# A gated delta rule on one core: the chunks' inverses applied to the decayed keys beforehand

## The chip, the core and the metric

The kernel runs on one core of a Trainium2 chip. A core has a matrix engine (TensorE, PE in the profile; PEld is its weight load, which overlaps the matmuls), three vector-like engines (VectorE or DVE, ScalarE or ACT, GpSimd or POOL), SyncE (SP), which issues most transfers, and 16 DMA engines that move data between device memory and the on-chip memory. Matmuls write to PSUM, a small memory of banks; DVE and ACT read the results from there. Each engine works through its own queue in order, and engines wait for one another by semaphores. The metric is device time in microseconds (us) for one launch.

## The reference, cut to what matters

The program is one step of a decoder layer for a prompt of 512 tokens (with 16 learned meta tokens ahead of it) and for eight sampled sequences of 8 tokens each. It has a differential attention, a gated delta rule, a merge of both by gates, and a convolutional feed-forward part. The change is in the delta rule, whose recurrence over chunks is this:

```python
lower = where(strict, einsum('cd,ed->ce', kb, kc) * decay, 0)
a_mat = lower + eye(chunk)
rhs = concatenate([vc * beta, kb * exp(gcum)], axis=-1)
sol = triangular_solve(a_mat, rhs, lower=True, unit_diagonal=True)
u, w = sol[..., :dv], sol[..., dv:]

def step(s, xs):
    v_new = u_i - w_i @ s
    intra = (q_i @ k_i.T) * dec_i
    o = (q_i * exp(g_i)) @ s + intra @ v_new
    s = s * exp(g_last) + (k_i * exp(g_last - g_i)).T @ v_new
    return s, o
```

There are four heads, each with keys and values of 128 elements. `v_new` is the inverse of `a_mat` applied to (values - decayed keys times state). The inverse can be applied to the difference, or to both of its terms; the reference does the second.

## The kernel before, in words

The kernel takes the prompt in chunks of 128 tokens (not 64 as the reference does), four per head, with the small inverse of each chunk built on the chip. The eight samples and the meta tokens form a fifth, shorter tile of 80 rows, called the tail, which is handled ahead of the four chunks and gives the first state `S`.

The projections are split into high and low parts and run as three matmuls each (`ps_d`, `ps_t`, `ps_g` and `ps_s` in the profile are the PSUM banks by tag, which late stages share). The delta rule's own small products are plain f32 matmuls, and each shows as two records.

The Python generators are streams: each `yield` hands over to another stream, and `yield DELAY[n]` says how much estimated work (in us) should be issued before the stream goes on. `merge` takes the stream that is furthest behind its weight and whose delay has passed. `main()` runs the prompt's attention, then `gdn`, then `mix_parts`; `rest()` runs the attention of the samples over the paged cache (page loads by SP, transpositions, scores, and products with `page` tiles) and then 16 gate projections (L1483). In `gdn`, the chain of head h (`gdn_chain`) is merged with the projections of head h+1 (`gdn_project`, with the convolution on DVE). For head 3 there is no next projection. The tile framework sets the waits, assigns the buffers, and may put an instruction that is ready ahead of others on its engine: for example the next head's `gu` (L714, POOL) runs in the solve of the head before it.

The steps of `gdn_chain` in order: `gu` and the decays (L714 to L745), transpositions and scaling of keys and values into `kn` and `vn` (L756 to L785), transposition of the keys into `kk` (L792, L796), the keys scaled for the state update in place as `kp` (L798 on DVE for the tail, L799 on POOL for the chunks), the scaled queries `qs` (L803, L804), the base blocks of the inverse (`gdn_base`), the doubling of the blocks (`gdn_solve`, which leaves the transposed inverse in `res["y"][:, i, 1]`), the tail, and then the chunk loop. In that loop, per chunk: the state times the keys, `kk` x `S`, in a bank; on DVE the negative decay and the values make `rhs` (L878); the inverse times `rhs`; a copy on ACT to `v` (L888); the state update `kp` x `v` and its sum on DVE (L893); and the two products of the output in a bank, read by ACT (L899) and DVE (L900). In chunk 1, `states()` puts the samples' state updates in between (L870 on DVE). After the loop POOL issues the state's transfer (L903) and computes a root for the output norm (`gf`, L376), after which the outputs are scaled, transposed and gated.

Buffers that matter here: `dd` is one tile per head pool (used by `gu`, by the decay differences, and by the solve), `on` is one tile (the outputs, five slots), `grhs`, `gv` and `gS` have two each, and the PSUM tag g has two banks in this stage.

Of the kernel before, what the change touches and what calls it, by code (L numbers as in the profile page):

```python
# [13 lines left out]
ALU = mybir.AluOpType  # L14
# [39 lines left out]
def _lay_out_constants():  # L54
# [78 lines left out]
DELAY = (  # L133
    10.08, 5.4, 0.6, 0.6, 6.0, 1.3, 0.9, 0.85, 1.32, 1.0, 1.68, 0.17, 26.0, 0.67, 2.93, 0.77,
    0.09, 0.85, 0.38, 2.28, 0.05, 1.54, 0.74, 1.56, 6.12, 0.84, 1.4, 11.52, 1.4, 1.68, 10.28,
)
# [14 lines left out]
class Body:  # L151
# [550 lines left out]
    def gdn_chain(self, h, st):  # L702
        nc, pool, a, o = self.nc, self.gpool, self.a, self.o
        q, kt, vt = st["q"], st["kt"], st["vt"]
        C4 = [128, 4, 128]

        def cols(ap, h=h):
            return ap[:, 0:4, h : h + 1].to_broadcast(C4)
# [6 lines left out]
            out=gu, in0=self.c("upper").unsqueeze(1).to_broadcast(C4), in1=cols(self.g), op=ALU.mult  # L715
# [9 lines left out]
        for big, sign in (("big_low", -1.0), ("big_up", 1.0)):  # L725
            m = self.t(pool, [NTL, NTL], "dt" + big)
            nc.vector.scalar_tensor_tensor(
                out=m, in0=rt[:NTL, :NTL], scalar=self.gc[:NTL, 4, h : h + 1], in1=self.c(big + "_t", NTL),
                op0=ALU.subtract, op1=ALU.add,
# [6 lines left out]
        dd = self.t(pool, C4, "dd")  # L736
# [13 lines left out]
        kn = self.t(pool, [128, 5, 128], "kn")  # L750
        vn = self.t(pool, [128, 5, 128], "vn")
# [20 lines left out]
        for i in range(4):  # L772
# [5 lines left out]
            out=rr, in0=rr, in1=self.mhalf[:, :10].rearrange("p (a b) -> p a b", a=2), op=ALU.pow  # L778
# [7 lines left out]
            out=kn[:, 0:4], in0=kn[:, 0:4], in1=kc[:, 0:4].unsqueeze(2).to_broadcast(C4), op=ALU.mult  # L786
        )
        yield DELAY[4]
        p = self.ps("t")
        self.transpose(p[:, :NTL], kn[:NTL, 4])  # L790
        kk = self.t(pool, [128, NT], "kk")
        nc.scalar.copy(kk[:, CS:NT], p[:, :NTL])  # L792
        p = self.ps4("t")
# [2 lines left out]
        nc.scalar.copy(kk[:, 0:SEQ].rearrange("p (c t) -> p c t", c=4), p)  # L796
        kp = kn
        nc.vector.tensor_scalar(kp[:NTL, 4], kn[:NTL, 4], self.ek[:NTL, 4, h : h + 1], None, op0=ALU.mult)  # L798
        nc.gpsimd.tensor_tensor(out=kp[:, 0:4], in0=kn[:, 0:4], in1=cols(self.ek), op=ALU.mult)  # L799
        yield DELAY[5]  # L800

# [2 lines left out]
        nc.gpsimd.tensor_tensor(out=qs[:, 0:SEQ], in0=q[:, 0:SEQ], in1=er[:, 0:SEQ], op=ALU.mult)  # L804
        yield 0.0

        on = self.t(pool, [128, 5, 128], "on")
        so = self.t(pool, [128, 5], "so")
        nc.vector.memset(so, 1.0)
        res = {}  # L810
# [7 lines left out]
        y, at = res["yt"], res["att"]  # L818
        p = self.ps("g")
        for b in range(NB):  # L820
# [3 lines left out]
        rhs = self.t(pool, [128, 128], "grhs", bufs=2)  # L824
        nc.vector.scalar_tensor_tensor(
            out=rhs[:64], in0=p[:64, :128], scalar=self.neg_eg[:64, 4, h : h + 1], in1=vn[:64, 4],
            op0=ALU.mult, op1=ALU.add,
# [5 lines left out]
        p = self.ps("g")  # L833
# [4 lines left out]
        p = self.ps("g")  # L838
        self.mm(p[:, :128], kp[64:NTL, 4], v[64:NTL], start=True, stop=True)
        S = self.t(pool, [128, 128], "gS", bufs=2)  # L840
        nc.vector.tensor_copy(S, p[:, :128])
        p = self.ps("g")
# [5 lines left out]
            out=state,  # L848
            in0=state,
            in1=last[:, 4:12].unsqueeze(2).to_broadcast([128, NB, 128]),  # L850
            op=ALU.mult,
        )
        vms = []
        for half in range(2):
# [3 lines left out]
                out=vm[:64],  # L858
                in0=v[:64].unsqueeze(1).to_broadcast([64, 4, 128]),
                in1=self.c("blocks_s", 64)[:, b4].unsqueeze(2).to_broadcast([64, 4, 128]),  # L860
                op=ALU.mult,
# [4 lines left out]
        def states():  # L866
            for b4, vm in vms:
                hp = self.ps4("g")
                self.mm(hp, kp[:64, 4], vm[:64].rearrange("p b v -> p (b v)"), start=True, stop=True)
                nc.vector.tensor_tensor(out=state[:, b4], in0=state[:, b4], in1=hp, op=ALU.add)  # L870


        for i in range(4):
            sl = slice(128 * i, 128 * i + 128)
            p = self.ps("g")
            self.mm(p[:, :128], kk[:, sl], S, start=True, stop=True)
            rhs = self.t(pool, [128, 128], "grhs", bufs=2)
            nc.vector.scalar_tensor_tensor(  # L878
                out=rhs, in0=p[:, :128], scalar=self.neg_eg[:, i, h : h + 1], in1=vn[:, i], op0=ALU.mult, op1=ALU.add
            )  # L880
            yield DELAY[9]
            if i == 1:
                states()
                yield 0.0
            p = self.ps("g")
            self.mm(p[:, :128], res["y"][:, i, 1], rhs, start=True, stop=True)
            v = self.t(pool, [128, 128], "gv", bufs=2)
            nc.scalar.copy(v, p[:, :128])  # L888
            yield DELAY[10]
            p = self.ps("g")  # L890
            self.mm(p[:, :128], kp[:, i], v, start=True, stop=True)
            S2 = self.t(pool, [128, 128], "gS", bufs=2)
            nc.vector.scalar_tensor_tensor(  # L893
                out=S2, in0=S, scalar=last[:, i : i + 1], in1=p[:, :128], op0=ALU.mult, op1=ALU.add
            )
            p = self.ps("g")
            self.mm(p[:, :128], qs[:, sl], S, start=True, stop=False)
            self.mm(p[:, :128], res["at"][:, i], v, start=False, stop=True)
            nc.scalar.activation(junk, p[:, :128], AF.Square, scale=cq[:, i : i + 1], accum_out=so[:, i : i + 1])  # L899
            nc.vector.tensor_copy(on[:, i], p[:, :128])  # L900
            S = S2
            yield DELAY[11]
# [7 lines left out]
            out=on[:, 0:4], in0=on[:, 0:4], in1=f[:, 0:4].unsqueeze(2).to_broadcast(C4), op=ALU.mult  # L910
# [4 lines left out]
        p = self.ps4("t")  # L915
# [4 lines left out]
        for dst, src in (((0, SEQ), p.rearrange("p c t -> p (c t)")), ((CS, CM), pt[:, 0:NS]), ((CM, NQ), pt[:, 78:80])):  # L920
            sl = slice(*dst)
            nc.vector.scalar_tensor_tensor(
                out=self.ob[:, h, sl], in0=src, scalar=self.gnorm, in1=z2[:, sl], op0=ALU.mult, op1=ALU.mult
# [878 lines left out]
```

## Time and profile before

| | us |
|---|---|
| median of 3 runs (1222.2 to 1225.16) | 1223.05 |
| the profiled execution | 1219.92 |
| its span, first to last instruction | 1218.2 |
| PE busy | 1168.2 (96%) |
| PEld busy | 1043.1 (86%) |
| DVE busy | 636.8 (52%) |
| ACT busy | 447.5 (37%) |
| POOL busy | 209.4 (17%) |

The mean granted TensorE clock is 0.992 of full speed. Busy times are those of one profiled execution. A matmul's end is modelled and matmuls overlap, so the distance between the starts of neighbours says more about PE's cost than the duration of one record. In rows grouped by line, the figures behind the bar are the busy time, the mean of one instruction in ns, and the idle time of the engine just before them with what ended it. In rows in order of time, the first number is the start, the second the duration (both in us), and the bracket at the end says how long the engine had been idle and what released it. The four chunk loops start at about 310, 404, 499 and 600 us.

### The profile page before, as it was taken

To read this page: it belongs to the slowest core of one execution; us is meant where nothing else is said; L and a number is where in the kernel's file an instruction comes from. 1 tells how busy PE (TensorE), PEld (TensorE's weight loads), DVE (VectorE), ACT (ScalarE), POOL (GpSimd) and SP (SyncE) were. 2 spreads that over 40 slices of the span, in tenths; PEclk is the share of its full clock that TensorE was granted. 3 is DMA by queue.
4 is the path that set the end of the run, shared out by engine and by line. 5 is a ranking of instruction groups with operands and counts; after the bars stand their busy time and mean duration, and the time that the engine had idled before them with its cause. 6 is when DMAs were issued, how large, how long until landed. Compare 5 with 4: busy or idle time off the path is not lost.

```text
span 1218.2 us, 24892 instructions
## 1 busy us (share of the span) xinstructions
PE 1168.2 (96%) x9439; PEld 1043.1 (86%) x9439; DVE 636.8 (52%) x1719; ACT 447.5 (37%) x1139; POOL 209.4 (17%) x341
## 2 busy tenths in 40 slices
PE   6999999989989989999999999999999999999996
PEld 5887787677677686679999987899999999999996
DVE  5456657586397497454226753455545545422224
ACT  5234444343333343342324433433333333323322
POOL 2122221150250241230100002321111111100000
PEclk9999999999999999999999999999999999999998
DMA  6374435726836657463232552322223223352222
GB/s 196 77 233 153 125 90 159 268 72 190 280 110 213 186 181 247 159 189 72 68 87 72 151 169 79 102 81 85 75 86 88 85 75 87 105 157 79 79 81 84
DMA packets 185006, 157.63 MB, mean 129 GB/s; under 512 B 13234, under 2 KB 147315, under 8 KB 184867
## 3 DMA queue, kind: packets, MB, share of 16 engines
q1 hardware_dynamic: 179569, 147.53, 40.0%
q0 software_dynamic: 4288, 5.16, 1.5%
q10 hardware_dynamic: 1030, 3.35, 0.8%
q8 instruction: 74, 1.21, 0.4%
q14 instruction: 45, 0.37, 0.1%
HBM read 146.12 MB, written 9.88 MB: 128 GB/s over the span
## 4 chain that ended last, share of the span: by engine, by line
PE 76%; DVE 7%; issue 6%; DMA 4%; ACT 3%; POOL 3%; DVEq 0%; ACTq 0%; POOLq 0%
PE ps_d L264 31%; PE ps_g L264 15%; PE ps_t L264 12%; PE ps_s L264 10%; PE ps_t L412 7%; DMA page<-in_cache_v 1%; PE ps_m L264 1%; DVE cy L640 1%; ACT KT L1388 1%; DMA wraw<-in_w_out 1%; DVE wlo L307 1%; DVE KT L1388 1%; DVE vt L647 1%; DMA wraw<-in_w_ffn_in 1%; DMA wraw<-in_w_in 0%
## 5 line engine op out<-in xcount | busy, mean ns | idle before, releaser
L307 DVE TENSOR_TENSOR wlo<-wraw,whi 128x512 fp32r<-128x512 f32 x238 | 159.0, 681 | 239.6 <-ACT whi L306 238.8
L306 ACT CAST whi<-wraw 128x512 fp32r<-128x512 f32 x240 | 143.1, 613 | 269.7 <-PE ps_d L264 106.5
L264 PE MATMUL ps_d<-xhi,whi 128*128 128x256 f32 (+2 forms) x704 | 219.7, 312 | 0.1
L264 PE MATMUL ps_d<-xhi,wlo 128*128 128x256 f32 (+2 forms) x704 | 215.0, 306 | 1.2 <-DVE wlo L307 1.2
L264 PE MATMUL ps_d<-xlo,whi 128*128 128x256 f32 (+2 forms) x704 | 215.2, 306 | 0.3 <-DVE xlo L307 0.2
L264 PEld LDWEIGHTS ps_d<-xhi,whi 128*128 128x128 f32 x704 | 135.3, 192 | 6.8 <-issue 4.6
L264 PEld LDWEIGHTS ps_d<-xhi,wlo 128*128 128x128 f32 x704 | 135.2, 192 | 5.0 <-issue 3.3
L264 PEld LDWEIGHTS ps_d<-xlo,whi 128*128 128x128 f32 x704 | 135.4, 192 | 3.9 <-issue 2.6
L412 PEld LDWEIGHTS ps_t<-consts,page 128*128 128x128 f32 x512 | 56.6, 142 | 25.2 <-issue 20.0
L412 PE MATMUL ps_t<-consts,page 128*128 128x128 f32 x512 | 75.7, 280 | 1.7 <-DVE KT L1388 0.8
L1388 ACT COPY KT<-ps_t 128x512 f32<-128x512 f32 x64 | 37.4, 585 | 83.1 <-PE ps_t L412 64.9
L1388 DVE COPY KT<-ps_t 128x512 f32<-128x512 f32 x64 | 44.0, 688 | 38.1 <-PE ps_t L412 33.4
L264 PE MATMUL ps_t<-fhi,whi 128*128 128x320 f32 (+2 forms) x208 | 62.1, 299 | 0.1
L264 PE MATMUL ps_t<-flo,whi 128*128 128x320 f32 (+2 forms) x208 | 61.3, 295 | 0.0
L264 PE MATMUL ps_t<-fhi,wlo 128*128 128x320 f32 (+2 forms) x208 | 61.1, 295 | 0.0
L264 PE MATMUL ps_g<-fhi,whi 128*128 128x320 f32 (+2 forms) x200 | 59.5, 298 | 0.0
L264 PE MATMUL ps_g<-flo,whi 128*128 128x320 f32 (+2 forms) x200 | 59.0, 295 | 0.0
L264 PE MATMUL ps_g<-fhi,wlo 128*128 128x320 f32 (+2 forms) x200 | 58.7, 294 | 0.0
L264 PE MATMUL ps_d<-fhi,whi 128*128 128x320 f32 (+2 forms) x192 | 57.4, 299 | 0.2 <-ACT fhi L306 0.2
L264 PE MATMUL ps_d<-flo,whi 128*128 128x320 f32 (+2 forms) x192 | 56.8, 296 | 0.0
L264 PE MATMUL ps_d<-fhi,wlo 128*128 128x320 f32 (+2 forms) x192 | 56.8, 296 | 0.0
L264 PE MATMUL ps_s<-KT,qb 128*32 128x256 f32 x512 | 46.2, 395 | 3.1 <-DVE KT L1388 2.2
(554 smaller groups left out, 2834.0 us busy)
## 6 DMA issues: line engine op xcount, KB each, us to landing
page<-in_cache_k SPq DMA_DIRECT2D x128, 256.0 KB, 4.3
page<-in_cache_v SPq DMA_DIRECT2D x128, 256.0 KB, 4.0
wraw<-in_w_in SPq DMA_DIRECT2D x88, 256.0 KB, 3.3
wraw<-in_w_ffn_in SPq DMA_DIRECT2D x88, 256.0 KB, 3.1
wraw<-in_w_down SPq DMA_DIRECT2D x40, 256.0 KB, 2.9
wraw<-in_w_out SPq DMA_DIRECT2D x16, 256.0 KB, 2.8
x<-in_x_prompt SPq DMA_DIRECT2D x4, 512.0 KB, 7.2
st<-in_state_gdn SPq DMA_DIRECT2D x4, 512.0 KB, 6.7
```

The source lines that it names most:

```text
L264: self.nc.tensor.matmul(out, lhsT, rhs, **kw)
L306: self.nc.scalar.copy(hi, raw)
L307: (eng or self.nc.vector).tensor_tensor(out=lo, in0=raw, in1=hi.bitcast(F32), op=ALU.subtract)
L412: self.nc.tensor.transpose(out, in_, self.ident[:k, :k])
L640: nc.vector.scalar_tensor_tensor(out=y, in0=pre[:, j : j + n], scalar=self.cw[:, ch, 24 + j : 25 + j], in1=y, op0=ALU.mult, op1=ALU.add)
L647: nc.vector.scalar_tensor_tensor(out=dst, in0=part(th), scalar=1.0, in1=part(y_), op0=ALU.add, op1=ALU.mult)
L1388: (nc.scalar.copy if j % 2 else nc.vector.tensor_copy)(kt[:, :, 128 * j : 128 * j + 128], tp)
```

## The change

The inverse is applied to both terms. Ahead of the loop, the keys are multiplied by the negative decay on POOL (`kne`, in the first four slots of `on`, which is allocated earlier for it), and after the tail four matmuls per head make the transformed decayed keys `wp`, which ACT copies to `wt` (a tile with the tag `dd`). In the loop, a chunk's values are the sum of two products in one bank: the inverse times `vn`, and `wt` times the state. The product of `kk` with the state and the scaled sum on DVE (L878) are gone. `yield DELAY[9]` stands once after the copy instead of once per chunk, and `states()` comes at the start of chunk 1 instead of between its `rhs` and its inverse.

```diff
@@ gdn_chain
         nc.vector.tensor_scalar(kp[:NTL, 4], kn[:NTL, 4], self.ek[:NTL, 4, h : h + 1], None, op0=ALU.mult)
+        on = self.t(pool, [128, 5, 128], "on")
+        kne = on[:, 0:4]
+        nc.gpsimd.tensor_tensor(out=kne, in0=kn[:, 0:4], in1=cols(self.neg_eg), op=ALU.mult)
         nc.gpsimd.tensor_tensor(out=kp[:, 0:4], in0=kn[:, 0:4], in1=cols(self.ek), op=ALU.mult)
...
-        on = self.t(pool, [128, 5, 128], "on")
         so = self.t(pool, [128, 5], "so")
...
+        wp = self.ps4("g")
+        for i in range(4):
+            self.mm(wp[:, i], kne[:, i], res["y"][:, i, 1], start=True, stop=True)
+        wt = self.t(pool, C4, "dd")
+        nc.scalar.copy(wt, wp)
+        yield DELAY[9]
         for i in range(4):
             sl = slice(128 * i, 128 * i + 128)
-            p = self.ps("g")
-            self.mm(p[:, :128], kk[:, sl], S, start=True, stop=True)
-            rhs = self.t(pool, [128, 128], "grhs", bufs=2)
-            nc.vector.scalar_tensor_tensor(
-                out=rhs, in0=p[:, :128], scalar=self.neg_eg[:, i, h : h + 1], in1=vn[:, i], op0=ALU.mult, op1=ALU.add
-            )
-            yield DELAY[9]
             if i == 1:
                 states()
                 yield 0.0
             p = self.ps("g")
-            self.mm(p[:, :128], res["y"][:, i, 1], rhs, start=True, stop=True)
+            self.mm(p[:, :128], res["y"][:, i, 1], vn[:, i], start=True, stop=False)
+            self.mm(p[:, :128], wt[:, i], S, start=False, stop=True)
             v = self.t(pool, [128, 128], "gv", bufs=2)
             nc.scalar.copy(v, p[:, :128])
```

## The prediction

> **What bounds the kernel now.** I read the page's engine shares first, then the table of busy time by stretch, then the order-of-time list of the delta rule's chunk loops (head 0 at 309 to 328 us, head 1 at 404 to 422.5, head 2 at 498.8 to 514.5, head 3 at 591 to 642), and last the chain of waits at a change of heads.
>
> ```profile
> span 1218.2 us, 24892 instructions
> PE 1168.2 (96%) x9439; PEld 1043.1 (86%) x9439; DVE 636.8 (52%) x1719; ACT 447.5 (37%) x1139; POOL 209.4 (17%) x341
> ```
> ```profile
> 240.00:540.00 300.00, 281.67 (x2776) 217.82 (x2777) 198.16 (x600) 114.08 (x326) 91.24 (x102) 0.99 0.60 186
> 540.00:660.00 120.00, 120.00 (x913) 117.73 (x912) 48.57 (x141) 38.52 (x99) 12.05 (x10) 1.00 0.29 74
> 340.00:380.00 40.00, 36.25 (x298) 27.57 (x297) 35.94 (x114) 16.68 (x49) 14.80 (x20) 1.00 0.49 146
> 420.00:460.00 40.00, 34.52 (x361) 30.25 (x353) 32.91 (x82) 16.75 (x55) 18.12 (x17) 0.96 0.68 217
> 309.00:328.00 19.00, 18.71 (x273) 12.83 (x274) 5.75 (x16) 4.10 (x14) 2.60 (x3) 1.00 0.89 301
> 404.00:422.50 18.50, 18.42 (x215) 13.49 (x214) 6.16 (x21) 7.09 (x19) 2.16 (x3) 1.00 0.47 135
> 498.80:514.50 15.70, 15.70 (x160) 10.93 (x158) 7.18 (x23) 7.16 (x19) 0.96 (x1) 1.00 0.33 98
> ```
> The columns are the stretch, its length, and PE, PEld, DVE, ACT and POOL busy, then clock and DMA. PE binds. In the chunk loops of heads 0 to 2 it lacks 0.29, 0.08 and 0.00 us; head 3's loop lies in a stretch without any gap. What PE leaves idle before 540 us (300 - 281.67 = 18.3 us) lies mostly elsewhere, at the heads' preparation, where DVE is busy 35.94 of 40 us. So a shorter chain inside the loop has next to no idle time to win: other streams (page matmuls, projections, gates) already fill it. What counts is the work that PE issues, and the small gaps each visit of the chain costs it.
>
> **The price of one small matmul.** From the order-of-time list, head 3 between the dense gate products:
>
> ```profile
> 637.90 0.31 PE L264 MATMUL ps_d<-xhi,wlo 128*128 128x322 f32 x1
> 638.05 0.39 PE L264 MATMUL ps_g<-grhs,xy 128*128 128x128 f32 x2
> 638.19 0.36 PE L264 MATMUL ps_d<-xhi,whi 128*128 128x256 f32 x1
> 638.39 0.28 PE L264 MATMUL ps_d<-xlo,whi 128*128 128x256 f32 x1
> ...
> 641.11 0.38 PE L264 MATMUL ps_g<-gv,kn 128*128 128x128 f32 x2
> 641.33 0.39 PE L264 MATMUL ps_g<-gS,er 128*128 128x128 f32 x2
> 641.55 0.39 PE L264 MATMUL ps_g<-gv,dbig_up 128*128 128x128 f32 x2
> ```
> Each 128x128x128 f32 product is two records. Three in a row start 0.22 us apart. A lone one costs the same here: 638.39 - 637.90 is 0.49 us, of which about 0.15 and 0.12 belong to the neighbours. So 0.22 us, with no extra for the visit.
>
> And from head 0's loop, where the neighbours are page matmuls:
>
> ```profile
> 309.85 0.30 PEld L264 LDWEIGHTS ps_g<-gS,kk 128*128 128x128 f32 x2 [0.20 <-issue]
> 309.86 0.49 PE L264 MATMUL ps_g<-gS,kk 128*128 128x128 f32 x2
> ...
> 310.27 1.52 PE L264 MATMUL ps_s<-page,pT 128*32 128x128 f32 x48
> 310.38 0.35 DVE L878 SCALAR_TENSOR_TENSOR grhs<-ps_g,neg_eg,vn 128x128 f32<-128x128 f32 x1 [0.33 <-PE ps_g L264]
> ```
> ```profile
> L264 PEld LDWEIGHTS ps_g<-gS,kk 128*128 128x128 f32 x32 | 4.9, 189 | 2.2 <-issue 1.6 <-DVE gS L893 0.4
> L264 PEld LDWEIGHTS ps_g<-grhs,xy 128*128 128x128 f32 x32 | 4.8, 188 | 3.9 <-DVE st L870 2.3 <-issue 1.0 <-DVE grhs L878 0.6
> ```
> Here the visit holds PE for 310.27 - 309.86 = 0.41 us, and the weight load stood 0.20 us before it. Over the 0.22 us of the product that is a gap of 0.2 us without the load's wait and 0.4 us with it. The group's row gives the number of such visits: 1.6 us of issue gaps at 0.20 us are 8 of the 16 visits of state times keys.
>
> **The change, part by part.** *Products.* Per chunk, state times keys goes and the transformed keys times state comes; inverse times rhs becomes inverse times vn: five products before and after. New are four per head, the decayed keys times the inverse: 16 x 0.22 = +3.5 us, on PE's path.
>
> *Visits.* Before, a chunk stops the fillers three times (keys, inverse, then three together), after it twice. Gone are 8 gaps of 0.4 = -3.2 us. Ends: 8 x 0.2 = -1.6, and all twelve of heads 0 to 2 at 0.4 = -4.8. The new group of four is one visit per head, with a gap in heads 0 to 2: +1.2 (0.6 at 0.2 each).
>
> *The scaled sum on DVE* (16 x 0.35 us, row L878 above) goes from chain and engine. PE waited for it 0.6 us in all: -0.6 (end: 0, if that wait goes over to the value's copy). The 2.3 us of waiting for the state update at L870 stays, since the state products still come ahead of chunk 1's bank. Otherwise the loop is merely shorter: kk.S at 309.86 to inverse at 311.72 is 1.9 us a chunk, which frees page matmuls for later, at the same cost to PE.
>
> ```profile
> 311.72 0.49 PE L264 MATMUL ps_g<-grhs,xy 128*128 128x128 f32 x2
> ```
> *The new copy on ACT* has the shape of the keys' copy below, 0.59 us, four times; ACT is 7.09 of 18.5 us busy in head 1's loop. The product before it takes one of two banks with tag g, which the tail's state frees only at 309.3 (row below), so it isn't early: about 309.4 + 0.9 for the products + 0.6 puts the first transformed product at 311.0, where the inverse stands now (311.72). The first chunk gains little; page matmuls cover it. Cost nothing beyond the PE terms.
>
> ```profile
> L796 ACT COPY kk<-ps_t x4: 573/585/600, 259.7 to 535.9; 128x512 f32<-128x512 f32 x4
> 309.02 0.29 DVE L841 COPY gS<-ps_g 128x128 f32<-128x128 f32 x1 [1.98 <-PE ps_g L264]
> ```
> *The new product on POOL* (keys times negative decay) is the shape of L799, 1.15 us, four times, issued just ahead of it. L799 waits for PE's transpositions, the new one only for the scaled keys, so it fits into that wait in heads 2 and 3, and behind it nothing on POOL moves by more than what is left:
>
> ```profile
> L799 POOL TENSOR_TENSOR kn<-kn,ek x4: 1039/1148/1309, 260.2 to 535.9; 128x512 f32<-128x512 f32 x4
> 446.87 1.25 POOL L799 TENSOR_TENSOR kn<-kn,ek 128x512 f32<-128x512 f32 x1 [1.49 <-PE ps_t L412]
> 535.87 1.31 POOL L799 TENSOR_TENSOR kn<-kn,ek 128x512 f32<-128x512 f32 x1 [4.63 <-PE ps_t L412]
> 263.16 0.90 POOL L953 TENSOR_TENSOR lbt<-dtbig_low,consts 80x80 f32<-80x80 f32 x1 [1.94 <-DVE dtbig_low L937]
> 447.14 1.07 DVE L798 TENSOR_SCALAR kn<-kn,ek 80x128 f32<-80x128 f32 x1
> L798 DVE TENSOR_SCALAR kn<-kn,ek x4: 269/281/1073, 259.3 to 535.4; 80x128 f32<-80x128 f32 x4
> ```
> In head 0 POOL idles 1.94 us before its next use (L953). What can show is DVE beside it: L798 takes 0.28 us, but 1.07 beside the POOL product at 446.87, so 0.8 a head, 3.2 us at most, and 0 if it falls beside other operations. I take 0.5, nearer to 0, because one of four was stretched so. [...]
>
> *The buffer dd* (one tile). Its next user is now the new copy, so the next head's gu (L714), which POOL computes early, in the solve, waits until chunk 3 has read the copy. Then come the out DMA and gf's root on POOL:
>
> ```profile
> L714 POOL TENSOR_TENSOR dd<-consts,g x4: 1047/1089/1727, 240.5 to 491.1; 128x512 f32<-128x512 f32 x4
> 420.36 0.49 PE L264 MATMUL ps_g<-grhs,xy 128*128 128x128 f32 x2
> 422.83 0.56 POOL L903 DMA_DIRECT2D out_new_gdn_prompt<-gS  x1 [7.71 <-DVE gS L893]
> 423.63 1.20 POOL L376 TENSOR_TENSOR gf<-gf,mhalf 128x5 f32<-128x5 f32 x1 [0.24 <-DVE gf L375]
> 425.91 0.70 PE L412 MATMUL ps_t<-consts,on 128*128 128x128 f32 x5 [0.99 <-DVE on L909]
> 426.66 1.06 PE L264 MATMUL ps_g<-dd,consts 128*128 128x512 f32 x2
> ```
> The last read stands where the inverse is now (420.36 to 420.85); gu fits in before 422.83, even at 1.73 us. Its reader comes at 426.66. Cost 0.
>
> Sum: 3.5 + 1.2 - 3.2 - 0.6 + 0.5 = +1.4 us. Ends: 3.5 + 0.6 - 4.8 - 0.6 = -1.3, and 3.5 + 1.2 - 1.6 + 3.2 = +6.3. The profiled execution took 1219.92 us (span 1218.2); it would take 1221.3. The median of the runs shown, 1223.05, stands 3.1 above it, so the same step gives 1224.4.
>
> **The rivals.** *Gains outside the loop (faster).* The fillers saved in the loops may go into the next head's preparation, where PE idles 3.75 us (340 to 380) and 5.48 us (420 to 460); if a third of the 18.3 us is filled, -6.1 + 1.4 = -4.7, 1218.4 us. For it: the loops become 5 to 7 us shorter (four times 1.9, less the 0.9 + 0.6 us ahead of the first chunk). Against it: in these stretches DVE is the full engine (35.94 and 32.91 of 40), and page transpositions need its copies.
>
> *gu ahead of gf (slower).* At head changes PE waits for the chain through gf (0.99 us before 425.91). If POOL issues gu less than its 1.73 us ahead of gf's input, gf and with it the next head start up to 1.7 us late, three times: +5.2 + 1.4, 1229.6 us. It decides once the last transformed product ends later than 421.9 (423.63 - 1.73). Against it: 1.0 us of slack by the rows above.
>
> *DVE held beside POOL (slower).* If each new POOL product costs DVE its whole 1.15 us where DVE binds, 4.6 takes the place of 0.5: +5.5, 1228.5 us. For it: 1.07 at 447.14. Against it: three of the four L798 kept to about 0.28 us. [...]
>
> That the chain isn't made faster at all is no rival: the forecast rests on a shorter chain that is worth nothing.
>
> **How the numbers follow.** 0.3% (3.7 us) is about what a measurement of this kernel can tell from no change: 1219.4 to 1226.7 us. Forecast (small loss or nothing; its own range 1220 to 1227): 0.50. Fillers into preparation: 0.22. gu ahead of gf: 0.16. DVE held: 0.12. So faster 0.22, same 0.50, slower 0.28. The range reaches to just past the two outer cases, 1217.5 to 1230, and takes in both ends of the sum (1221.7 and 1229.4).
>
> **What would show it.** PE with 32 more records; the group for decayed keys times inverse at about 0.22 us each; two visits per chunk, with issue gaps ahead of the keys' loads gone; loops 5 to 7 us shorter in heads 0 to 2; PE still without a gap from 540 to 660 us; L714 after the last chunk instead of in the solve; preparation stretches with the same PE idle. I'm wrong if the idle of 240 to 540 us moves by more than 3 us either way, if head 3's loop had gaps to win, or if gf starts later behind its input than the 0.24 us of now.

## The result, and the profile after

The changed kernel takes 1254.64 us (median of 4 runs, 1254.15 to 1257.14), the kernel before beside it 1224.11 us (1222.20 to 1226.14). These medians lie 30.5 us apart. The recorded ratio of the two is 1.0275, with a 95% interval of 1.0247 to 1.0303: 2.7% slower, about 33 us, and this is the loss that the shares below are taken of. The forecast was 1224.4 us, and its range ended at 1230.

The page's head and the table of busy time by stretch, after:

```profile
span 1253.0 us, 24964 instructions
PE 1181.3 (94%) x9471; PEld 1053.4 (84%) x9471; DVE 635.7 (51%) x1703; ACT 448.1 (36%) x1143; POOL 215.7 (17%) x345
```
```profile
240.00:540.00 300.00, 274.68 (x2541) 212.33 (x2540) 188.63 (x565) 107.11 (x305) 90.31 (x96) 0.97 0.52 164
540.00:660.00 120.00, 105.34 (x909) 98.45 (x910) 40.40 (x124) 32.59 (x88) 15.08 (x13) 0.93 0.38 103
340.00:360.00 20.00, 16.46 (x118) 15.23 (x117) 16.04 (x41) 9.96 (x39) 9.13 (x14) 0.85 0.19 55
360.00:380.00 20.00, 16.67 (x132) 12.19 (x130) 16.21 (x64) 3.85 (x8) 5.57 (x8) 0.90 0.55 163
520.00:540.00 20.00, 17.98 (x180) 11.95 (x179) 9.53 (x34) 10.36 (x31) 7.53 (x7) 0.83 0.47 155
540.00:560.00 20.00, 13.89 (x236) 9.61 (x236) 10.71 (x48) 4.59 (x16) 8.16 (x7) 0.97 0.89 283
560.00:580.00 20.00, 11.45 (x65) 11.00 (x66) 8.46 (x38) 3.42 (x11) 0.56 (x1) 0.61 0.17 40
```
The same view of the kernel before, for the stretches that the prediction did not show:

```profile
360.00:380.00 20.00, 19.20 (x176) 12.65 (x176) 18.00 (x67) 6.47 (x12) 4.60 (x7) 1.00 0.77 237
540.00:560.00 20.00, 20.00 (x153) 19.97 (x153) 15.47 (x72) 5.49 (x14) 3.95 (x3) 1.00 0.32 80
560.00:580.00 20.00, 20.00 (x164) 19.80 (x162) 5.38 (x10) 5.87 (x14) 1.00 (x1) 1.00 0.29 69
```
The span grew by 34.8 us: PE is busy 13.1 us longer (1181.3 - 1168.2) and idle 21.7 us longer (71.7 against 50.0). The idle time is all in the delta rule. From 240 to 540 us PE idles 25.3 us where it idled 18.3 (+7.0), and from 540 to 660 us 14.7 us where it idled 0 (+14.7). 540 to 580 us was full of gate products before; now PE works 25.3 of these 40 us, 11.5 of them (560 to 580 us) at a granted clock of 0.61. The clock explains most of the busy time as well. With 1 less the clock as the share lost, the four stretches after with a clock of 0.90 or less lose 16.46 x 0.15 + 16.67 x 0.10 + 17.98 x 0.17 + 11.45 x 0.39 = 11.7 us; the kernel before lost 1.4 us in this way (34.52 x 0.04, 420 to 460 us). That estimate of 10.3 us and the 3.5 us of new products make the 13.1, roughly.

What PE waits for between 557 and 571 us is seen in the order of time, PE and then DVE, after:

```profile
557.41 0.43 PE L264 MATMUL ps_s<-page,pT 128*32 128x128 f32 x8 [0.31 <-DMA page<-in_cache_v]
566.46 0.64 PE L264 MATMUL ps_t<-pv,consts 128*32 128x128 f32 x4 [8.62 <-DVE pv L1443]
569.19 0.45 PE L412 MATMUL ps_t<-consts,oS 128*128 128x128 f32 x1 [2.09 <-ACT gt L1486]
...
571.57 0.41 PE L264 MATMUL ps_d<-xlo,whi 128*128 128x256 f32 x1
571.78 0.41 PE L264 MATMUL ps_d<-xhi,wlo 128*128 128x256 f32 x1
...
575.78 0.28 PE L264 MATMUL ps_d<-xhi,whi 128*128 128x256 f32 x1
575.90 0.28 PE L264 MATMUL ps_d<-xlo,whi 128*128 128x256 f32 x1
```
```profile
555.03 0.17 DVE L969 STREAM_SHUFFLE row<-xc 128x10 f32<-128x10 f32 x1
...
565.33 0.68 DVE L981 TENSOR_TENSOR xy<-xc,consts 128x512 f32<-128x512 f32 x1
565.93 0.47 DVE L1443 TENSOR_SCALAR pv<-ps_s,rc 128x256 f32<-128x256 f32 x1
```
None of this is code that the diff touches. `pv` is the end of the samples' attention: the last page product of a pair of samples is at 557.41 us, DVE scales the sum (L1443), PE multiplies it, and after every second pair a head norm and a transposition of `oS` follow; only then do the next gate products (`ps_d`) come in PE's queue, which has none between 485.3 and 571.2 us. Between 555.03 and 565.9 us DVE works through the base blocks of head 3, a chain of short dependent operations on `row` and `xc`, and `pv` stands behind them. The kernel before had it the other way round, 8.6 us ahead of the same loop:

```profile
534.17 0.48 DVE L1440 TENSOR_SCALAR pv<-ps_s,rc 128x256 f32<-128x256 f32 x1 [1.82 <-PE ps_s L264]
...
542.78 0.17 DVE L966 STREAM_SHUFFLE row<-xc 128x10 f32<-128x10 f32 x1
```
So the samples' stream (pages, `pv`, head norm, gates) is late against the main stream. Main's weight in this stage is so large that it is taken whenever it is ready, so the other stream is issued while main waits out a `yield DELAY[n]`. DELAY[9] is 1.0. The change leaves one such yield where there were four: by the program's own estimate, 3 us less of other work is issued per head. The group row of `pv`, before and after, gives the second pair's start and the last pair's (first and last of the three in this part):

```profile
L1440 DVE TENSOR_SCALAR pv<-ps_s,rc x3: 468/483/485, 333.0 to 534.2; 128x256 f32<-128x256 f32 x3
```
```profile
L1443 DVE TENSOR_SCALAR pv<-ps_s,rc x3: 474/477/485, 355.7 to 565.9; 128x256 f32<-128x256 f32 x3
```
The second pair's is 22.7 us later, and the last pair's 31.7 us. That is not a sum of 3 us per head: the stream falls behind in jumps.

### The profile page after: what moved, and what is told of

It is laid out like the page before. It is cut to its first block, busy times and chain, and to the rows that moved or that the text cites. A ratio compares the mean times of both kernels' runs of the same rounds, so it can differ in the third digit from the quotient of the medians.

```text
span 1253.0 us, 24964 instructions
## 1 busy us (share of the span) xinstructions
PE 1181.3 (94%) x9471; PEld 1053.4 (84%) x9471; DVE 635.7 (51%) x1703; ACT 448.1 (36%) x1143; POOL 215.7 (17%) x345
## 4 chain that ended last, share of the span: by engine, by line
PE 67%; issue 15%; DVE 9%; POOL 3%; ACT 3%; DMA 2%; DVEq 0%; ACTq 0%; POOLq 0%
PE ps_d L264 26%; PE ps_g L264 14%; PE ps_t L264 10%; PE ps_s L264 9%; PE ps_t L412 7%; DMA page<-in_cache_v 1%; DVE cy L640 1%; PE ps_m L264 1%; ACT KT L1391 1%; DVE wlo L307 1%; POOL grr L777 1%; DVE KT L1391 0%; DVE xc L971 0%; ACT whi L306 0%; POOL hss L376 0%
```

## Experiments

Theory T: the loss comes from the timetable of the streams, the yields that went, and not from the instructions. Rival I: it comes from the new instructions or their buffers. Ratios are to the kernel before, run on the same chip.

**The yields given back (e1).** The changed kernel with a yield per chunk as before. The work of the four new products is booked one per chunk, ahead of the yield, where the kernel before booked its product of keys and state (with them, 24 small products are booked per head, where the kernel before books 20):

```diff
         nc.scalar.copy(wt, wp)
-        yield DELAY[9]
+        self.work -= 4 * 1.68e-3 * 128
         for i in range(4):
             sl = slice(128 * i, 128 * i + 128)
+            self.work += 1.68e-3 * 128
+            yield DELAY[9]
```


> The changed kernel with the old timetable of the streams: DELAY[9] is yielded once per chunk again, and the estimated work is booked where the old kernel booked it (per chunk one small product more, four less after the copy). Its instructions are those of the changed kernel, all of them. Theory A (the change itself costs little; the loss comes from the sample attention falling behind the delta rule, so that the end of its second and fourth pair, the scaling pv on DVE, lands in or behind the base blocks of heads 1 and 3): 1225 to 1229 us, with the PE idle of 520 to 580 us back from 16.7 to under 4 us, and pv of the fourth pair ahead of head 3's base blocks. Theory B (the new instructions or buffers themselves cost it: POOL product, copy, tile dd, extra matmuls): 1245 us or more.

Measured 1234.26 us, ratio 1.0111 (1.0079 to 1.0143). Some 60% of the loss is gone with the new instructions all in place. The last pair's `pv` is at 546.7 us, 8.6 us ahead of head 3's base blocks (555.3), and PE idles 1.6 us from 540 to 580 us, as expected. The time is not: it was to be 1229 us at most, and where the other 40% lies was not settled.

**The kernel before, with less delay (e2, e8).** No instruction is added; one number falls, the delay behind the base-block loop's issue in each head (DELAY[12]):

```diff
-    ... 1.68, 0.17, 26.0, 0.67, ...
+    ... 1.68, 0.17, 22.0, 0.67, ...
```


> The kernel before with one number changed: the delay after the base blocks (DELAY[12]) is 22 instead of 26, so that each head's chain takes 4 us less of the other streams with it; not one instruction is added or removed. Theory A: it loses as the changed kernel did, 1240 to 1256 us, with PE idle of some 10 us or more in head 3's base blocks. Theory B: 1222 to 1227 us, no loss, since none of the new instructions is in it.

> The kernel before with DELAY[12] 24 instead of 26, between the kernel before and run e2. On DVE's queue only the third and fourth pair's ends now stand behind the base blocks, the second pair's end stays where it was. Theory A: the loss is made mostly by the fourth pair's end in head 3, 10 to 25 us above the kernel before, less than e2's 30. Theory B: no loss.

With 22: 1249.30 us, ratio 1.0241 (1.0205 to 1.0277). With 24: 1252.50 us, ratio 1.0250 (1.0199 to 1.0302). PE in order of time, the kernel before with 24:

```profile
564.25 0.64 PE L264 MATMUL ps_t<-pv,consts 128*32 128x128 f32 x4 [8.19 <-DVE pv L1440]
566.99 0.45 PE L412 MATMUL ps_t<-consts,oS 128*128 128x128 f32 x1 [2.09 <-ACT gt L1483]
```
These are the two gaps of the changed kernel (8.62 and 2.09), in a kernel that has nothing of the change. Two us less per head is enough, and four cost no more than two: a step, not a slope (with 24 there are two runs). The expectation that 24 loses less than 22 fell.

Where the step lies is seen at the third pair, DVE in order of time, in the kernel before and then with 24:

```profile
457.19 0.47 DVE L1440 TENSOR_SCALAR pv<-ps_s,rc 128x256 f32<-128x256 f32 x1
...
459.17 0.17 DVE L966 STREAM_SHUFFLE row<-xc 128x10 f32<-128x10 f32 x1
```
```profile
456.76 0.17 DVE L966 STREAM_SHUFFLE row<-xc 128x10 f32<-128x10 f32 x1
...
475.43 0.48 DVE L1440 TENSOR_SCALAR pv<-ps_s,rc 128x256 f32<-128x256 f32 x1 [4.51 <-PE ps_s L264]
```
With 24 the second pair is still where it was (334.8 us, before 333.0). The third goes from 2.0 us ahead of head 2's base-block loop to 18.7 us behind its start, and there it waits for its page products (`ps_s`), not for DVE. In every run here that loses 2.4% or more (the changed kernel, e2, e4, e6, e8, e9) the third pair's `pv` starts behind the start of head 2's loop; in all the others it is ahead. Not run: the kernel before with three yields of DELAY[9] less and nothing else. e2 and e8 stand for it by another delay.

**The changed kernel, with more delay (e3, e7).** The same number, 26 to 30 and to 32:

> The changed kernel with DELAY[12] 30 instead of 26, everything else as changed: the four us that the chunk loop no longer hands to the other streams are handed out in the base blocks. Theory A: 1225 to 1230 us. Theory B: 1250 us or more, since the chain is only made longer.

> The changed kernel with DELAY[12] 32 instead of 26 (run e3 had 30). Theory A, with what is left over being the added work alone: 3 to 6 us above the kernel before, better than e3 if e3's rest was timetable, the same as e3 (7 to 10 us above) if it was the change itself.

With 30: 1227.79 us, ratio 1.0068 (1.0041 to 1.0094). With 32: 1233.68 us, ratio 1.0093 (1.0064 to 1.0122). With 30, three quarters of the loss are gone, by one number far from the diff. PE's and DVE's rows of it:

```profile
PE 1171.9 (96%) x9471; PEld 1047.8 (85%) x9471; DVE 633.8 (52%) x1703; ACT 449.9 (37%) x1143; POOL 215.4 (18%) x345
```
```profile
540.17 0.48 DVE L1443 TENSOR_SCALAR pv<-ps_s,rc 128x256 f32<-128x256 f32 x1 [2.72 <-PE ps_s L264]
548.77 0.17 DVE L969 STREAM_SHUFFLE row<-xc 128x10 f32<-128x10 f32 x1
```
`pv` is 8.6 us ahead of head 3's base blocks again, the granted clock is 1.00 from 540 to 580 us, and PE is busy 3.7 us more than before. That is near the new products' 3.5, but it doesn't measure them: e12 below, which has none of them, is busy 3.9 us more (1172.1). With 32 the loss is no smaller than with 30 (the intervals overlap), so e7 does not tell whether e3's rest is timetable or change.

**The kernel before, with more delay (e12).**

> The kernel before, with the delay of the base-block loop at 28 instead of 26. Theory (a threshold: 24 and 22 fall behind it by some 28 us, 26 stands ahead of it): no loss, within 4 us of the kernel before, with pair 4's pv still ahead of head 3's base-block loop. If the time were to go with the size of the delay and 26 was just the best of a smooth curve, it would be slower by 5 us or more.

1229.38 us, ratio 1.0073 (1.0049 to 1.0098). The expectation fell: `pv` is ahead of the base blocks (539.4 us), and the kernel still loses 0.7%. So of the four values tried (22, 24, 26, 28) 26 is the best for the kernel before, with a small loss on one side and a step on the other. So the 0.7% which e3 keeps need not be the new work's price alone; the delay of 30 may carry a part of it.

**The price of the added work (e5, e10, e11).** The kernel before with the new work, its result unused and without any booked work, so that the yields stay as they are: both parts (e5), POOL's product alone (e10), four products per head and their copy alone (e11). The core of e11, and the line of e10:

```diff
+        wp = self.ps4("g")
+        for i in range(4):
+            nc.tensor.matmul(wp[:, i], vn[:, i], res["y"][:, i, 1], start=True, stop=True)
+        wt = self.t(pool, C4, "dd")
+        nc.scalar.copy(wt, wp)
```
```diff
+        nc.gpsimd.tensor_tensor(out=kne, in0=kn[:, 0:4], in1=cols(self.neg_eg), op=ALU.mult)
```


> The kernel before with only the added work of the change, its result unused: the POOL product of keys and negative decay, four small matmuls per head with the inverse, and the copy on ACT into dd, none of it booked as estimated work, so that the streams keep the old timetable. The old chunk loop with keys times state and the scaled sum stays. Theory A: PE busy up by 16 x 0.22 = 3.5 us, the time 3 to 6 us above the kernel before. Theory B (the added instructions or the held buffer cost more than their work, the rest of run e3's 8 us included): 8 us or more above.

> The kernel before, with only the new product on POOL (keys times the negative decay, into the tile of the outputs, unused). Added work of both kinds cost 7 to 8 us where 3.5 us of it are matmuls; this tells where the rest is. If POOL's product delays the keys for the state update, or holds DVE beside it in the preparation: +2 to +5 us, with PE idle more at 340 to 380 and 440 to 480 us. If it hides in POOL's wait, as the prediction had it: within 1 us of the kernel before.

> The kernel before, with only the four extra products per head and their copy on ACT into dd (the values in the keys' place, result unused, no booked work). Price by the prediction: 16 x 0.22 = 3.5 us and 0.6 to 1.2 us for four more visits, 4 to 5 us in all. If it is 7 to 8 us, the copy, its bank or the buffer dd carry the rest; if it is about 3.5 us, the visits cost nothing and the rest belongs to POOL's product.

Both: 1229.04 us, ratio 1.0069 (1.0043 to 1.0094). POOL's product alone: 1220.91 us, ratio 1.0006 (0.9989 to 1.0023). The products alone: 1225.68 us, ratio 1.0040 (1.0024 to 1.0055). The products and their copy cost about 4.9 us (2.9 to 6.7, the interval times 1220), an interval that takes in the 3.5 to 4.7 of the prediction's terms for products and visits, and POOL's product nothing that shows. The two sum to 0.46%, the combined kernel has 0.69%; the intervals overlap. Rival I is left with 5 to 8 us of the 33 (e11, e5), and by the upper end of e5 with 11. The other place of `states()` was not tried by itself; e1 and e3 have it too.

**The buffer dd (e4).** The changed kernel with a tile of its own for the copy:

```diff
-        wt = self.t(pool, C4, "dd")
+        wt = self.t(pool, C4, "wt")
```


> The changed kernel with a tile of its own for the transformed keys instead of dd, so that the next head's gu is no longer held until the last chunk has read it. Theory A: 1252 to 1257 us, no change. The rival of the prediction (gu ahead of gf, or gu too late for the next head): 1240 us or less if that is the main cause, 2 to 5 us less if it is part of it.

1253.41 us, ratio 1.0269 (1.0225 to 1.0312). No difference that shows; two runs leave some 5 us open either way.

**Which wait holds PE at 557 to 571 us (e6, e9).** If it is DVE's queue alone, taking the samples' end off DVE must give the time back. e6 scales `pv` of pairs 2 and 4 on ACT and makes the low parts of the first two gates' weights on POOL; e9 moves the head norm as well:

```diff
-            nc.vector.tensor_scalar(pv, acc[:, :256], rs, None, op0=ALU.mult)
+            if pr % 2:
+                nc.scalar.activation(pv, acc[:, :256], AF.Identity, scale=rs)
+            else:
+                nc.vector.tensor_scalar(pv, acc[:, :256], rs, None, op0=ALU.mult)
...
+            nc.gpsimd.tensor_scalar(ss, ss, 1.0 / 128, EPS, op0=ALU.mult, op1=ALU.add)
+            nc.gpsimd.tensor_tensor(out=ss, in0=ss, in1=self.mhalf[:rows, :nh], op=ALU.pow)
+            nc.scalar.activation(on[:, 0], on[:, 0], AF.Identity, scale=ss)
+            nc.gpsimd.tensor_tensor(out=on[:, 0], in0=on[:, 0], in1=self.sub[:rows], op=ALU.mult)
```


> The changed kernel with the work of the second and fourth pair's end and of the first two gates' weights taken off DVE's queue: the scaling pv of these pairs runs on ACT, the low parts of the two gates' weights on POOL. The timetable stays as changed, so the pair still ends beside head 3's base blocks. Theory A1 (PE idles there because pv and the weights' low parts queue behind the base blocks on DVE): the idle of 540 to 580 us falls from 14.7 us to under 5, the time by 9 to 15 us, to 1239 to 1245. Theory A2 (PE idles there because the pages and the weights arrive late, whatever DVE does): 1250 to 1255 us.

> The changed kernel, with every step between the last page product of sample pairs 2 and 4 and the gates taken off DVE: the scaling of pv on ACT, the head norm's mean and root on POOL, its scaling on ACT and its weight on POOL, and the low parts of the first two gates' weights on POOL. Theory (the loss around 550 us is DVE's in-order queue: these steps stand behind head 3's base-block loop): the gaps of 8.6 and 2.1 us ahead of the products on pv and ahead of the head norm's transposition shrink to under 2 us together, the granted clock of 560 to 580 us comes back from 0.61 to above 0.9, and the time falls by 9 to 20 us against the changed kernel (1254), to 1234 to 1245. Rival (PE has simply too little other work left at that place, whichever queue holds pv): the same idle time turns up in 540 to 600 us behind another wait, and the time stays at 1250 to 1256.

e6: 1255.85 us, ratio 1.0270 (1.0226 to 1.0315). e9: 1252.67 us, ratio 1.0268 (1.0233 to 1.0303). Neither gains. e6's time is near what its A2 gives, but the wait in its rows is for `oS` on DVE, not for pages or weights. PE in order of time, e6 and then e9, and the stretches of e9:

```profile
560.54 0.41 PE L265 MATMUL ps_t<-pv,consts 128*32 128x128 f32 x4 [0.59 <-ACT pv L1445]
570.89 0.45 PE L413 MATMUL ps_t<-consts,oS 128*128 128x128 f32 x1 [9.94 <-DVE oS L1344]
```
```profile
556.87 0.41 PE L265 MATMUL ps_t<-pv,consts 128*32 128x128 f32 x4 [0.60 <-ACT pv L1451]
559.98 0.48 PE L413 MATMUL ps_t<-consts,oS 128*128 128x128 f32 x1 [2.70 <-POOL oS L1346]
565.14 0.33 PE L413 MATMUL ps_t<-consts,xyt 80*80 80x80 f32 x1 [4.69 <-DVE xyt L976]
```
```profile
440.00:460.00 20.00, 13.99 (x201) 11.40 (x199) 16.34 (x45) 5.00 (x12) 13.54 (x11) 0.91 0.47 131
540.00:560.00 20.00, 13.42 (x237) 9.42 (x236) 11.23 (x49) 6.62 (x23) 9.37 (x10) 0.95 0.83 274
560.00:580.00 20.00, 15.04 (x91) 14.59 (x92) 7.29 (x33) 2.72 (x7) 0.00 (x0) 0.70 0.13 31
```
In e6 the gap ahead of `pv` is gone (0.59), and the head norm, still on DVE behind the base blocks, holds PE 9.94 us instead. In e9 both gaps together are 3.30 us, and now PE waits 4.69 us for the base blocks themselves: `xyt`, head 3's inverse, stands in PE's queue ahead of the next gate products. PE's idle time from 540 to 580 us goes from 14.7 to 11.5 us only, and head 2's preparation is worse (440 to 460 us: PE busy 13.99 of 20, in the changed kernel 16.89). Some 2.5 us of the low parts moved to POOL lie there; that they are the reason is not shown. So the reading "DVE's queue holds PE" is right for the wait at the head of the row, but no sufficient cause: once the samples' stream is late, each wait that is removed uncovers another, because the next gates come behind all of it. That is nearer to e9's rival (too little other work is left at that place, whichever queue holds `pv`) than to its theory. Which of the three waits would have to go last was not settled. And both runs leave the third pair alone: in e9 its `pv` starts at 477.1 us, as late as in the changed kernel (476.7). What bringing that pair forward would give back was not tried.

## Why the prediction was wrong, point by point

**The step that failed** is the sentence under the scaled sum: the loop is merely shorter, "which frees page matmuls for later, at the same cost to PE", with "a shorter chain inside the loop has next to no idle time to win" behind it. It treated the other streams' work as a stock that is used whenever there is room. It is issued by main's yields. The change removes three of them per head, the front of this document said so, and the sum had no term for it. What the runs put in its place: two us less per head in the kernel before cost 2.5% (e8), and the change's loss comes back to 0.7% by another delay (e3). The prediction had named the signs itself: idle of 240 to 540 us moving by more than 3 us (it moved by 7.0), and PE without a gap from 540 to 660 us (it idles 14.7 us there).

**Products, +3.5 us: right.** Four products follow one another without a gap, after:

```profile
307.85 1.16 PE L264 MATMUL ps_g<-xy,on 128*128 128x128 f32 x8
```
Less the end of the last, about 0.28 us, that is 0.22 us each, and e11's price with their copy (2.9 to 6.7 us) takes in the 3.5.

**Visits, -3.2 and +1.2 us, and the wait for rhs, -0.6: seen in part, and worth nothing that shows.** The group of inverse times values, after:

```profile
L264 PEld LDWEIGHTS ps_g<-vn,xy 128*128 128x128 f32 x32 | 4.8, 188 | 4.1 <-DVE st L872 3.0 <-issue 0.4 <-PE ps_s L264 0.2
```
Issue gaps fell from 1.6 + 1.0 us to 0.4, and the wait for `rhs` (0.6) is gone, 2.8 us in all. The loads of the new group have 0.2 us of issue gaps where the prediction put +1.2, and the wait for the samples' state at L872 grew from 2.3 to 3.0. Against that, the kernels that have it (the changed one, e1, e3, e7) all lie 8 us or more above the one before. If the gain is there, the streams' shift in each of them hides it.

**Loops 5 to 7 us shorter: wrong.** From the tail's copy to the last chunk's, head 0, before and after:

```profile
308.01 0.26 ACT L836 COPY gv<-ps_g 80x128 f32<-80x128 f32 x1
...
326.47 0.27 ACT L888 COPY gv<-ps_g 128x128 f32<-128x128 f32 x1 [1.16 <-PE ps_g L264]
```
```profile
306.00 0.26 ACT L838 COPY gv<-ps_g 80x128 f32<-80x128 f32 x1
...
324.55 0.28 ACT L891 COPY gv<-ps_g 128x128 f32<-128x128 f32 x1
```
18.5 us in both; between the same copies head 1 became 1.7 us shorter and head 2 0.3 us longer. The chain's steps are fewer, and the loop is not: the prediction took the old distances of the chain for its limit, which nothing here bears out.

**DVE beside POOL, +0.5 us: right in price, wrong in shape.** In e10 three of the four L798 are stretched (two in the changed kernel), and the time is not:

```profile
L798 DVE TENSOR_SCALAR kn<-kn,ek x4: 281/1060/1091, 259.7 to 537.3; 80x128 f32<-80x128 f32 x4
```
The median of L798 went from 0.28 to 1.06 us, 0.78 us more, and the kernel's time by 0.06%. So the rival of 4.6 us, which assumed that DVE loses POOL's whole 1.15 us in each head, has the longer L798 in the trace and no price that shows here: e10's interval, -1.3 to +2.8 us, takes in the 0.5 and not the 4.6.

**The buffer dd and gu ahead of gf, 0 us: right.** `gu` moved behind the last chunk, as predicted, and it is over before `gf`'s input is made (POOL and DVE, after):

```profile
526.85 1.04 POOL L714 TENSOR_TENSOR dd<-consts,g 128x512 f32<-128x512 f32 x1 [4.80 <-PE ps_g L264]
528.98 0.16 DVE L375 TENSOR_SCALAR gf<-so 128x5 f32<-128x5 f32 x1
529.23 1.20 POOL L376 TENSOR_TENSOR gf<-gf,mhalf 128x5 f32<-128x5 f32 x1
```
`gf` starts 0.25 us behind the start of its input's step, before and after, at all three changes of heads. So its rival (1229.6 us) does not occur; e4 agrees, but would not by itself exclude 5 us.

**The direction.** The prediction gave 0.28 to slower, for two reasons that do not hold. The mechanism that decided was not among its rivals.

Of the 33 us, 5 to 8 are the new work (e11 and e5), and with a delay moved all but 8 come back (e3). Whether e3's 8 are all new work stays open: e12's delay of 28 alone cost the kernel before as much. No version here beats the kernel before.

## What to carry to other kernels

Where streams are interleaved by booked delays, a diff that takes out a yield changes how much of every other stream has been issued at each later point; price it as a term of its own, by asking which long step of another engine the other stream's end must come ahead of. Before a change in such a kernel is judged, move one delay by a few us in both kernels: if the unchanged one loses as much, as it did here, what was measured may be the timing shift and not the change's work. And a wait that stands in front of PE is not the whole cause until its removal has been tried: here the first was taken away, then the second, and the time stayed.

## What the runs showed of the hardware

In the changed kernel the gap of 8.62 us cost PE more than its length. After, by stretch:

```profile
530.00:535.00 5.00, 3.25 (x17) 2.31 (x20) 3.56 (x15) 3.11 (x6) 0.90 (x2) 0.63 0.56 209
566.00:571.00 5.00, 2.45 (x14) 2.00 (x14) 3.19 (x11) 2.51 (x8) 0.56 (x1) 0.50 0.26 57
571.00:576.00 5.00, 5.00 (x25) 5.00 (x26) 0.00 (x0) 0.27 (x1) 0.00 (x0) 0.53 0.40 100
```
After the gap of 8.62 us the granted clock is 0.50, and the gate products start 0.21 us apart (571.57, 571.78) until full speed returns at about 575.6 us, from where they start 0.12 us apart (575.78, 575.90). That is 9 us after PE resumed at 566.46, and 6.4 us after its last gap ended (569.19). In e2 and e8, behind nearly the same two gaps (8.79 and 8.19 us, then 2.09 us in both), it came 4.7 and 7.9 us after the last one. In the first row the clock is low without such a gap: it averaged 0.63 where PE was busy 3.25 of 5 us, and the longest gap was 1.25 us:

```profile
531.49 1.25 PE L412 MATMUL ps_t<-consts,on 128*128 128x128 f32 x5 [1.25 <-DVE on L912]
```
So a gap far shorter than the long one went with a lowered clock here. It need not: a sparser stretch of e11, with a gap of 1.69 us, kept the full clock, as its row by stretch and PE's row in it show:

```profile
435.00:440.00 5.00, 2.81 (x19) 2.25 (x18) 3.65 (x12) 3.65 (x15) 4.32 (x6) 1.00 0.25 59
```
```profile
439.37 0.33 PE L412 MATMUL ps_t<-consts,q 128*128 128x128 f32 x1 [1.69 <-ACT gjunk L761]
```
What makes the difference, no run here tells.
